# Mixers' and embedding's transposes by VectorE and DRAM into dense tiles, 64-row products in alternating halves, gate columns later

## The chip, the core and the metric

The kernel runs on one core of one Trainium2 chip. The metric is the device time of one launch in microseconds, as the median of repeated runs. PE is TensorE's matmul queue and PEld its weight loads; DVE is VectorE, ACT ScalarE, POOL GpSimd, SP the engine whose queue issues all DMA transfers here.

## The reference, cut to what matters

Two layers run over 256 tokens of width 1024. Each layer is a feed-forward half step, two token mixers side by side, a second feed-forward half step and a gated embedding:

```
x = x + 0.5 * swiglu(rmsnorm(x), ffn1)
z = rmsnorm(x) @ w_in                 # mlstm q,k,v,o,i,f ; swa q,k,v ; gates ga, gb
A = (sigmoid(o) * rmsnorm(mlstm(q,k,v,i,f))) @ w_a   # 4 heads, q and k 64 wide, v 128 wide
B = attention(rms(q), rms(k), v, window 128, sinks) @ w_b   # 8 q heads, 2 kv heads, 64 wide
x = x + (sigmoid(ga) * A + sigmoid(gb) * B) @ w_out
x = x + 0.5 * swiglu(rmsnorm(x), ffn2)
x = x + sigmoid(rmsnorm(x) @ w_ple_gate) * (p[i] @ w_ple)
```

## The kernel before, in words

The 256 tokens are two tiles (t = 0, 1) of 128 partitions. Every weight product runs in three matmuls (L230 to L232): weights and activations are split into a high and a low part (`hi`, `lo`), and high times low, low times high and high times high are summed in PSUM. Weights come as units of 1 MB. `load_next` issues a unit's DMA into one of three buffers (`raw`), ScalarE casts the high part (L202) and VectorE subtracts it for the low part (L203) into one of four buffers. `take` keeps four units ahead, so the DMA of a unit waits until VectorE is done with the unit three before, and its cast waits until PE is done with the unit four before. `stream` runs a unit for both token tiles; one tile's share is 12 matmuls of 512 columns, and behind each share `tick()` moves every waiting generator by one `yield`.

All small work of the mixers sits in such generators. A `W_` number counts the ticks that a generator waits before its next step, and so it sets how many shares of weight matmuls PE has between asking for a result and using it. PE's instructions stand in the order of the code; VectorE, ScalarE and SP run their own queues in an order that a scheduler wrote when the program was built. Each queue runs in order: a waiting instruction holds all that stand behind it.

The stages of the mixers are the projections sq, if, mqk, mv, mo, ga0, ga1, gb0, gb1 (28 ticks from mqk on), then the products with `w_a` (`ya`) and `w_b` (`yb`), then `w_out`. Beside the projections run two chains. The attention chain: normalise q and k, transpose them (`tps`, `tpk`), logits (`lg`, 64 rows of contraction, kv head 0 in partitions 0 to 63 and kv head 1 in 64 to 127), bias and softmax on DVE and ACT, transpose the probabilities (`pt`), multiply by v (`ov`), transpose the result (`tp_hb`) into `abT`. The mLSTM chain: transpose q and k (`tpq`), gates in rows, a matrix of decays `E01`, `E2` times the products of q and k (`st`, 64 rows), times v (`num`), normalise, gate, transpose (`tp_ha`) into `abT`. `drain()` runs what is left of both chains before `ya`.

Those transposes are PE instructions with the identity, followed by a copy out of PSUM. The feed-forward stages already transpose in another way (`turn`, L256): VectorE transposes 32 x 32 blocks (`inq`), SP writes them to DRAM (`scr`), SP reads them back in the wanted order (`back`), and a copy or a split moves `back` to its place.

Of the kernel before, what the change touches and what calls it, by code (L numbers as in the profile page):

```python
# [8 lines left out]
F32 = mybir.dt.float32  # L9
# [43 lines left out]
W_NORM = 5  # L53
W_CP = 6
# [6 lines left out]
W_HA = 5  # L61
# [3 lines left out]
def trunk_kernel(ctx: ExitStack, tc: tile.TileContext, a: dict, out: bass.AP):  # L65
# [99 lines left out]
    for i in range(DEPTH):  # L165
        specs.extend(ffn_specs(a["ffn1_wi"][i], a["ffn1_wo"][i], f"f1{i}"))
        for z, cols in Z.items():
            specs.extend(by_cols(a["w_in"][i], D, cols, f"z{i}_{z}"))
        for n in range(2):
            cols = [(512 * n, 512 * (n + 1))]  # L170
            specs.extend(by_cols(a["w_a"][i], 512, cols, f"wa{i}_{n}"))
            specs.extend(by_cols(a["w_b"][i], 512, cols, f"wb{i}_{n}"))
# [343 lines left out]
    def mix_in(pool, i, xn, finish):  # L516
# [21 lines left out]
        qk = pair([P, 10, HD], "qk")  # L538
# [3 lines left out]
        qT = pool.tile([P, 2, S], F32, name=f"qT{i}")  # L542
        kT = pool.tile([P, 2, S], F32, name=f"kT{i}")
# [3 lines left out]
        ha = pair([P, MLH, P], "ha")  # L547
# [20 lines left out]
        def ep_mqk(t, o, rstd):  # L568
            z = work.tile([P, 512], F32, tag="sg", name=f"mqk{i}_{t}")
            nc.scalar.activation(z, o, AF.Copy, scale=rstd)  # L570

            def turn():
                yield
                tp = bank(f"tpq{i}_{t}")
                for b in range(4):
                    nc.tensor.transpose(tp[:, b * P : (b + 1) * P], z[:, b * P : (b + 1) * P], ident)
                tv = tp.rearrange("p (b s) -> p b s", s=P)
                tok = slice(t * P, (t + 1) * P)
                nc.vector.tensor_copy(qT[:, :, tok], tv[:, 0:2, :])
                nc.vector.tensor_scalar(kT[:, :, tok], tv[:, 2:4, :], HD**-0.5, None, ALU.mult)  # L580

            spawn(turn())
# [12 lines left out]
        def swa(t):  # L595
            for _ in range(t):
                yield
            sq = pool.tile([P, 10, HD], F32, tag="s4", name=f"sqk{i}_{t}", bufs=4)
            nc.scalar.activation(sq, qk[t], AF.Square)
            s10 = small.tile([P, 10], F32, tag="s10", name=f"s10_{i}_{t}")  # L600
            nc.vector.reduce_sum(s10, sq, axis=AX.X)
            v10 = small.tile([P, 10], F32, tag="v10", name=f"v10_{i}_{t}")
            nc.vector.tensor_scalar(v10, s10, 1.0 / HD, EPS, ALU.mult, ALU.add)
            r10 = small.tile([P, 10], F32, tag="r10", name=f"r10_{i}_{t}")
            pow_neg_half(r10, v10, 10)
            z = pool.tile([P, 5 * P], F32, tag="s4", name=f"qkn{i}_{t}", bufs=4)
# [14 lines left out]
            for _ in range(W_NORM):  # L621
                yield
            tp = bank(f"tps{i}_{t}")
            for j in range(4):
                nc.tensor.transpose(tp[:, j * P : (j + 1) * P], z[:, j * P : (j + 1) * P], ident)
            nc.scalar.activation(qTs[t], heads(tp, P), AF.Copy, scale=qs)
            tk = bank(f"tpk{i}_{t}")
            nc.tensor.transpose(tk[:, 0:P], z[:, 4 * P :], ident)
            nc.scalar.activation(kTs[:, t * P : (t + 1) * P], tk[:, 0:P], AF.Copy, scale=qg[:, 1:2])
            for h0 in range(0, SWQ, 4 * (2 - t)):  # L630
                spawn(swa_part(t, h0))

        def swa_part(t, h0):
# [3 lines left out]
            nh = SWQ if t == 0 else SWQ // SWKV  # L637
            part = slice(h0, h0 + nh)
# [5 lines left out]
            yield  # L644
            L = pool.tile([P, nh, nk], F32, tag="s4", name=f"L{nmp}", bufs=4)
            mx = stat("mx")
            for j0 in range(0, nh, per):
                g = (h0 + j0) // 4
                rows = slice(HD * g, HD * (g + 1))
                o = heads(bank(f"lg{nmp}_{j0}"), nk)  # L650
                for j in range(per):
                    nc.tensor.matmul(
                        o[:, j, :], qTs[t][rows, (h0 + j0 + j) % 4, :], kTs[rows, 0:nk], start=True, stop=True
                    )
                js = slice(j0, j0 + per)
                nc.vector.tensor_tensor(L[:, js, :], o, bias[:, h0 + j0 : h0 + j0 + per, boff:], op=ALU.add)
                nc.vector.reduce_max(mx[:, js], L[:, js, :], axis=AX.X)
# [18 lines left out]
            for kt in range(t + 1):  # L676
                for j0 in range(0, nh, 4):
                    tp = bank(f"pt{nmp}_{kt}_{j0}")
                    for j in range(4):
                        nc.tensor.transpose(  # L680
                            tp[:, j * P : (j + 1) * P], L[:, j0 + j, kt * P : (kt + 1) * P], ident
                        )
                    dst = PT[:, kt, j0 : j0 + 4, :]
                    if kt + j0 == 0:
                        nc.scalar.copy(dst, heads(tp, P))
                    else:
                        nc.vector.tensor_copy(dst, heads(tp, P))
# [20 lines left out]
            hi, lo = abT[t][1]  # L708
            transpose_split(hb, nh * HD // P, hi[:, ks, :], lo[:, ks, :], f"hb{nmp}")
# [10 lines left out]
        ln, lf, F, c, M, emt = (row(n) for n in ("ln", "lf", "F", "c", "M", "emt"))  # L720

        def ml_gates():
# [19 lines left out]
            nc.vector.scalar_tensor_tensor(lf, gf, 0.0, F, ALU.min, ALU.subtract)  # L742
            nc.vector.tensor_tensor(lf, lf, c, op=ALU.add)
            nc.vector.tensor_tensor_scan(F, ones4, lf, 0.0, op0=ALU.mult, op1=ALU.add)
# [4 lines left out]
            for _ in range(W_CP):  # L749
                yield  # L750
            cp = bank(f"cp{i}")
# [5 lines left out]
            tc.keep_in_program_order(nc.sync.dma_start(scr, M))  # L757
            for _ in range(W_MB):
                yield
            spread = bass.AP(tensor=s0.tensor, offset=s0.offset, ap=[[0, P], [S, MLH], [1, S]])  # L760
            tc.keep_in_program_order(nc.sync.dma_start(Mb, spread))

        def ml_mix():
# [12 lines left out]
            for par in range(2):  # L776
                rows = slice(HD * par, HD * (par + 1))
                o = bank(f"st0{i}_{par}").rearrange("p (h t s) -> p h t s", t=2, s=P)
                for hh in range(2):
                    nc.tensor.matmul(o[:, hh], kT[rows, hh, 0:P], qT[rows, hh, :], start=True, stop=True)  # L780
                for hh in range(2):
                    ev = E01[:, 0:2, 2 * hh + par, :]
                    nc.vector.tensor_tensor(ev, ev, o[:, hh], op=ALU.mult)
                o = heads(bank(f"st1{i}_{par}")[:, 0 : 2 * P], P)
                for hh in range(2):
                    nc.tensor.matmul(o[:, hh], kT[rows, hh, P:S], qT[rows, hh, P:S], start=True, stop=True)
                for hh in range(2):
                    ev = E2[:, 2 * hh + par, :]
                    nc.vector.tensor_tensor(ev, ev, o[:, hh], op=ALU.mult)
            for t in range(NT):  # L790
                yield
                spawn(ml_out(t, E01, E2))

        def ml_out(t, E01, E2):
# [5 lines left out]
            jn = pool.tile([P, P], F32, tag="jn", name=f"jn{i}_{t}", bufs=1)  # L800
# [33 lines left out]
            hi, lo = abT[t][0]  # L834
            transpose_split(haf, 4, hi, lo, f"ha{i}_{t}")
# [81 lines left out]
    for i in range(DEPTH):  # L917
# [6 lines left out]
        with tc.tile_pool(name=f"ple{i}", bufs=1, side="right", reuse_waits="tile") as pool:  # L924
            pT = [halves(pool, 2, f"pT{i}_{t}") for t in range(NT)]

            def embed(_):
# [5 lines left out]
                for t in range(NT):  # L933
                    transpose_split(pin[t], 2, pT[t][0], pT[t][1], f"p{i}_{t}")
# [85 lines left out]
```

## Time and profile before

| | |
|---|---|
| median of three runs | 1127.14 us (1127.10 to 1127.16) |
| the profiled execution's own time | 1129.26 us |
| its span | 1127.5 us |
| PE busy in the span | 1117.9 us (99%) |
| DVE, ACT busy | 731.2 us (65%), 586.2 us (52%) |
| chain of work that ended last | PE 98%, DVE 1% |

The profiled execution took 2.1 us more than the median run, of which 1.8 us lie outside its span. A busy PE counts a matmul until its modelled end, and neighbours overlap, so the mean of one matmul is not what it costs; the distance from one start to the next is.

### The profile page before, as it was taken

Reading aid. Unit: us, or ns where it says so; the run is one execution under the profiler, and the core shown is the slowest. Engines: PE = TensorE matmul, PEld = TensorE weight load, DVE = VectorE, ACT = ScalarE, POOL = GpSimd, SP = SyncE. Lnnn points to the kernel's source line nnn. Section 1 sums busy time; section 2 is a strip of 40 time slices with the busy share of each in tenths; the row PEclk is TensorE's granted clock in tenths of the full one; section 3 lists DMA queues with packets and bytes.
Section 4 is the critical chain, followed back from the end, with each engine's and each line's share of the span. In section 5 each row is a group of like instructions: output and inputs, shape, how many; then the busy total and the mean of one; then the engine's idle time right before and its main releaser. Section 6 shows DMA issues by size and latency. Waiting matters only on the chain.

```text
span 1127.5 us, 13561 instructions
## 1 busy us (share of the span) xinstructions
PE 1117.9 (99%) x5220; PEld 929.3 (82%) x5220; DVE 731.2 (65%) x924; ACT 586.2 (52%) x848; POOL 30.5 (3%) x30
## 2 busy tenths in 40 slices
PE   8999999999999999999999999999999999999998
PEld 6788888888888888888888888888888888888887
DVE  5775755686676667656676666557846766667554
ACT  6543544667645544434664454447865364445442
POOL 1000000100000000000000000001000000000000
PEclk9999999999999999999999999999999999999999
DMA  7887766643554767756657776665544557776661
GB/s 256 277 278 248 247 214 198 224 168 113 179 191 151 261 217 246 256 190 230 208 177 246 256 238 207 224 201 188 170 148 154 193 185 226 247 238 228 218 205 38
DMA packets 147489, 235.05 MB, mean 208 GB/s; under 512 B 13288, under 2 KB 51296, under 8 KB 147424
## 3 DMA queue, kind: packets, MB, share of 16 engines
q1 hardware_dynamic: 147424, 234.19, 63.2%
q8 instruction: 41, 0.67, 0.2%
q14 instruction: 24, 0.20, 0.1%
HBM read 219.46 MB, written 14.70 MB: 208 GB/s over the span
## 4 chain that ended last, share of the span: by engine, by line
PE 98%; DVE 1%; DMA 0%; ACT 0%; issue 0%; SPq 0%
PE h_f L231 14%; PE h_f L230 14%; PE h_f L232 14%; PE acc_f_o L230 7%; PE acc_f_o L231 7%; PE acc_f_o L232 7%; PE z_mix_ga L230 1%; PE z_mix_ga L232 1%; PE z_mix_ga L231 1%; PE acc_wout L230 1%; PE z_mix_gb L230 1%; PE acc_wout L232 1%; PE z_mix_gb L232 1%; PE acc_wout L231 1%; PE z_mix_gb L231 1%; PE acc_pg L230 1%
## 5 line engine op out<-in xcount | busy, mean ns | idle before, releaser
L203 DVE TENSOR_TENSOR lo_f<-raw_f,hi_f 128x1024 fp32r<-128x1024 f32 (+1 forms) x176 | 207.6, 1216 | 97.6 <-ACT hi_f L202 97.6
L202 ACT CAST hi_f<-raw_f 128x1024 fp32r<-128x1024 f32 (+1 forms) x178 | 176.5, 1039 | 157.0 <-PE h_f L232 96.6
L203 DVE TENSOR_TENSOR lo_f_o<-raw_f_o,hi_f_o 128x1024 fp32r<-128x1024 f32 x88 | 104.2, 1219 | 73.6 <-ACT hi_f_o L202 73.6
L231 PE MATMUL h_f<-hi_f,xT_f_0l 128*128 128x512 f32 x352 | 137.8, 392 | 2.3 <-DVE xT_f_0l L247 2.3
L230 PE MATMUL h_f<-lo_f,xT_f_0h 128*128 128x512 f32 x352 | 138.6, 394 | 0.1
L230 PE MATMUL h_f<-lo_f,xT_f_1h 128*128 128x512 f32 x352 | 137.2, 390 | 0.6 <-DVE lo_f L203 0.5
L232 PE MATMUL h_f<-hi_f,xT_f_0h 128*128 128x512 f32 x352 | 137.5, 391 | 0.0
L232 PE MATMUL h_f<-hi_f,xT_f_1h 128*128 128x512 f32 x352 | 137.0, 389 | 0.0
L231 PE MATMUL h_f<-hi_f,xT_f_1l 128*128 128x512 f32 x352 | 137.0, 389 | 0.0
L202 ACT CAST hi_f_o<-raw_f_o 128x1024 fp32r<-128x1024 f32 x88 | 88.0, 1048 | 91.5 <-PE acc_f_o L232 55.0
L231 PEld LDWEIGHTS h_f<-hi_f,xT_f_0l 128*128 128x128 f32 x352 | 66.5, 189 | 16.0 <-DVE xT_f_0l L247 2.6
L230 PEld LDWEIGHTS h_f<-lo_f,xT_f_1h 128*128 128x128 f32 x352 | 66.1, 188 | 15.1 <-DVE lo_f L203 1.4
L230 PEld LDWEIGHTS h_f<-lo_f,xT_f_0h 128*128 128x128 f32 x352 | 66.4, 189 | 14.5 <-issue 0.6
L232 PEld LDWEIGHTS h_f<-hi_f,xT_f_0h 128*128 128x128 f32 x352 | 66.6, 189 | 14.0
L232 PEld LDWEIGHTS h_f<-hi_f,xT_f_1h 128*128 128x128 f32 x352 | 66.0, 188 | 13.7
L231 PEld LDWEIGHTS h_f<-hi_f,xT_f_1l 128*128 128x128 f32 x352 | 66.1, 188 | 13.5
L232 PE MATMUL acc_f_o<-hi_f_o,hT_f_1h 128*128 128x512 f32 x176 | 68.5, 389 | 0.0
L230 PE MATMUL acc_f_o<-lo_f_o,hT_f_0h 128*128 128x512 f32 x176 | 68.5, 389 | 0.0
L231 PE MATMUL acc_f_o<-hi_f_o,hT_f_0l 128*128 128x512 f32 x176 | 68.5, 389 | 0.0
L232 PE MATMUL acc_f_o<-hi_f_o,hT_f_0h 128*128 128x512 f32 x176 | 68.5, 389 | 0.0
L230 PE MATMUL acc_f_o<-lo_f_o,hT_f_1h 128*128 128x512 f32 x176 | 68.5, 389 | 0.0
L231 PE MATMUL acc_f_o<-hi_f_o,hT_f_1l 128*128 128x512 f32 x176 | 68.5, 389 | 0.0
(363 smaller groups left out, 2042.3 us busy)
## 6 DMA issues: line engine op xcount, KB each, us to landing
raw_f<-in_ffn_wi_dram SPq DMA_DIRECT2D x79, 1024.0 KB, 5.3
raw_f_o<-in_ffn_wo_dram SPq DMA_DIRECT2D x40, 1024.0 KB, 5.2
scr_h_f<-inq_h_f SPq DMA_DIRECT2D x40, 256.0 KB, 3.5
back_h_f<-scr_h_f SPq DMA_DIRECT2D x40, 256.0 KB, 4.4
raw_f<-in_ffn_wi_dram SPq DMA_DIRECT2D x18, 512.0 KB, 4.5
raw_z_ga<-in_w_in_dram SPq DMA_DIRECT2D x8, 1024.0 KB, 5.4
raw_z_gb<-in_w_in_dram SPq DMA_DIRECT2D x8, 1024.0 KB, 5.2
raw_wout<-in_w_out_dram SPq DMA_DIRECT2D x8, 1024.0 KB, 5.0
```

What stands on the lines that cost most here:

```text
L202: nc.scalar.copy(hi[:, o:e], raw[:, o:e])
L203: (nc.gpsimd if between and o // step % 2 == 0 else nc.vector).tensor_tensor(lo[:, o:e], raw[:, o:e], hi[:, o:e].bitcast(F32), op=ALU.subtract
L230: nc.tensor.matmul(o, xh, wl[:, k, sl], start=start, stop=False)
L231: nc.tensor.matmul(o, xl, wh[:, k, sl], start=False, stop=False)
L232: nc.tensor.matmul(o, xh, wh[:, k, sl], start=False, stop=stop)
```

## The change

`back_from` runs `turn` for the mixers' blocks, and what was a PE transpose and a copy out of PSUM becomes a VectorE transpose, two DMAs and a copy (or split) out of SBUF into the same dense tiles. Per layer this holds for `tps` and `tpk` (2 turns of 640 columns), `tpq` (2 of 512), `pt` (6 of 512), `tp_hb` (one of 512, two of 256), `tp_ha` (2 of 512) and the embedding's `tp_p` (2 of 256). The transposes of `x` (`tp_f`, `tp_mix`, `tp_ple`), of the merged mixers (`tp_mx`) and of the gates (`gp`, `cp`) stay with PE. The logits of both kv heads and the `st` products of both partition halves alternate, each half in its own PSUM bank. `scr0<-M` and its spread are issued before the gate columns (`cp`), `yb` comes before `ya`, and the waits in ticks are set anew. Some tiles share buffers (`qk` with `ha`, `lf` with `ln`).

```diff
-W_NORM = 5
-W_CP = 6
+W_NORM = 2
+W_MQ = 2
+W_ROW = 7
-W_HA = 5
+W_HA = 3
...
+        def back_from(src, name):
+            k = src.shape[1]
+            inq = work.tile([P, 5 * P], F32, tag="xg", name=f"inq_{name}")
+            back = pool.tile([P, 5 * P], F32, tag="back", name=f"back_{name}", bufs=2)
+            b = back[:, 0 : k * P].rearrange("p (a e) -> p a e", a=4)
+            yield from turn(inq, src, b, name)
+            return b.rearrange("p a (k s) -> p k a s", s=32)
...
-                        nc.tensor.transpose(
-                            tp[:, j * P : (j + 1) * P], L[:, j0 + j, kt * P : (kt + 1) * P], ident
-                        )
+                b = yield from back_from(src, f"PT{nmp}_{kt}_{j0}")
...
+            for k0 in range(0, 4, per):
+                os = [heads(bank(f"lg{i}_{t}_{k0}_{g}"), nk) for g in range(SWKV)]
+                for j in range(per):
+                    for g in range(SWKV):
+                        rows = slice(HD * g, HD * (g + 1))
+                        nc.tensor.matmul(
+                            os[g][:, j, :], qTs[t][rows, k0 + j, :], kTs[rows, 0:nk], start=True, stop=True
+                        )
...
-            transpose_split(hb, nh * HD // P, hi[:, ks, :], lo[:, ks, :], f"hb{nmp}")
+            yield from back_split(blocks(hb), hi, lo, f"hb{nmp}")
...
-            transpose_split(haf, 4, hi, lo, f"ha{i}_{t}")
+            yield from back_split(blocks(haf), *abT[t][0], f"ha{i}_{t}")
...
         for n in range(2):
+            ob = [bank(f"yb{i}_{t}_{n}") for t in range(NT)]
+            stream(ob, abTs, [f"wb{i}_{n}_0"], 4, kbase=4)
             oa = [bank(f"ya{i}_{t}_{n}") for t in range(NT)]
             stream(oa, abTs, [f"wa{i}_{n}_0"], 4)
-            ob = [bank(f"yb{i}_{t}_{n}") for t in range(NT)]
-            stream(ob, abTs, [f"wb{i}_{n}_0"], 4, kbase=4)
```

On PE, the products of mLSTM's q and k in layer 0 stood behind a transpose of attention's result and in one half after the other (`st00_0` and `st10_0` read partitions 0 to 63, `st00_1` and `st10_1` 64 to 127):

```order
L253 MATMUL tp_hb0_1_0_2267<-ident_85,hb0_1_0_2234 128x128 x2
L253 MATMUL tp_hb0_1_4_2272<-ident_85,hb0_1_4_2245 128x128 x2
L780 MATMUL st00_0_2277<-qT0_1561,kT0_1562 128x256 x2
L786 MATMUL st10_0_2282<-qT0_1561,kT0_1562 128x128 x2
L780 MATMUL st00_1_2287<-qT0_1561,kT0_1562 128x256 x2
L786 MATMUL st10_1_2292<-qT0_1561,kT0_1562 128x128 x2
```

These are the same products in the change:

```order
L807 MATMUL st00_0_2217<-qkT0_1561 128x256
L807 MATMUL st00_1_2218<-qkT0_1561 128x256
L807 MATMUL st00_0_2217<-qkT0_1561 128x256
L807 MATMUL st00_1_2218<-qkT0_1561 128x256
L815 MATMUL st10_0_2227<-qkT0_1561 128x128
L815 MATMUL st10_1_2228<-qkT0_1561 128x128
L815 MATMUL st10_0_2227<-qkT0_1561 128x128
L815 MATMUL st10_1_2228<-qkT0_1561 128x128
```

The transposes are gone from here, and the halves alternate product by product.

On DVE, in the stretch of gb0 in layer 0, this stood between attention's last product with v and the split of its transposed result (`hb0_1_0` and `hb0_1_4` are the two kv heads of token tile 1, `abT0_1_1l` is what `yb` of tile 1 reads):

```order
L702 TENSOR_TENSOR hb0_1_0_2234<-ov0_1_0_2225,rinv0_1_0_2042 128x256
L702 TENSOR_TENSOR hb0_1_4_2245<-ov0_1_4_2236,rinv0_1_4_2069 128x256
L247 TENSOR_TENSOR abT0_0_1l_1534<-tp_hb0_0_0_2218,abT0_0_1h_1533 128x512
L203 TENSOR_TENSOR lo_z0_gb0_0_2249<-raw_z0_gb0_0_2247,hi_z0_gb0_0_2248 128x1024 x2
L783 TENSOR_TENSOR E01_0_2190<-E01_0_2190,st00_0_2277 128x2x128 x2
L247 TENSOR_TENSOR abT0_1_1l_1538<-tp_hb0_1_0_2267,abT0_1_1h_1537 128x256
```

Now the same two ends stand farther apart, with both round trips of token tile 0 between them:

```order
L729 TENSOR_TENSOR hb0_1_4_2457<-ov0_1_4_2448,rinv0_1_4_2094 128x256
L264 STREAM_TRANSPOSE inq_ha0_0_2459<-ha0_0_2237 128x512
L264 STREAM_TRANSPOSE inq_hb0_1_0_2476<-hb0_1_0_2446 128x256
L248 TENSOR_TENSOR abT0_0_1l_1534<-back_hb0_0_0_2435,abT0_0_1h_1533 128x512
L204 TENSOR_TENSOR lo_wb0_0_0_2489<-raw_wb0_0_0_2487,hi_wb0_0_0_2488 128x1024 x2
L264 STREAM_TRANSPOSE inq_hb0_1_4_2479<-hb0_1_4_2457 128x256
L264 STREAM_TRANSPOSE inq_ha0_1_2484<-ha0_1_2238 128x512
L204 TENSOR_TENSOR lo_wa0_0_0_2535<-raw_wa0_0_0_2533,hi_wa0_0_0_2534 128x1024 x2
L248 TENSOR_TENSOR abT0_0_0l_1532<-back_ha0_0_2460,abT0_0_0h_1531 128x512
L204 TENSOR_TENSOR lo_wb0_1_0_2574<-raw_wb0_1_0_2572,hi_wb0_1_0_2573 128x1024 x2
L248 TENSOR_TENSOR abT0_1_1l_1538<-back_hb0_1_0_2477,abT0_1_1h_1537 128x256
L248 TENSOR_TENSOR abT0_1_1l_1538<-back_hb0_1_4_2480,abT0_1_1h_1537 128x256
```

What moved: the split for tile 1 of `yb` now stands behind two splits that wait for transfers from DRAM and behind six weight splits.

On SP, the queue held in this place only weights (`raw_`), one after another; now, in the same place of layer 0, it reads:

```order
L270 DMA scr_hb0_1_0_2507<-inq_hb0_1_0_2476 128x256
L199 DMA raw_wa0_1_0_2614<-in_w_a_dram 128x4x512
L270 DMA scr_hb0_1_4_2509<-inq_hb0_1_4_2479 128x256
L270 DMA scr_ha0_1_2511<-inq_ha0_1_2484 128x512
L274 DMA back_ha0_0_2460<-scr_ha0_0_2482 128x4x128
L274 DMA back_hb0_1_0_2477<-scr_hb0_1_0_2507 128x4x64
L199 DMA raw_wout0_0_2648<-in_w_out_dram 128x2x1024
L274 DMA back_hb0_1_4_2480<-scr_hb0_1_4_2509 128x4x64
```

Writes to and reads from DRAM stand between the weights, and a weight that waits for its buffer holds them.

## Rows read from the trace of the kernel before

**Rows 1.** The page: the chain that ended last, share of the span by engine.
```profile
PE 98%; DVE 1%; DMA 0%; ACT 0%; issue 0%; SPq 0%
```
**Rows 2.** The chain in order of time: start us, length us, what.
```profile
218.96 0.44 PE gp L727 x4
...
238.15 1.64 PE lg L652 x16
...
242.73 2.90 PE lg L652 x16
...
254.97 1.75 PE pt L680 x16
...
264.46 3.52 PE ov L694 x32
```
**Rows 3.** PE's transposes by form: count, then busy us and mean ns.
```profile
L680 PE MATMUL pt<-ident,L 128*128 128x128 f32 x48 | 5.9, 272 | 0.0
...
L625 PE MATMUL tps<-ident,qkn 128*128 128x128 f32 x16 | 2.4, 272 | 0.0
...
L253 PE MATMUL tp_p<-ident,pin 128*128 128x128 f32 x8 | 1.2, 271 | 0.0
L628 PE MATMUL tpk<-ident,qkn 128*128 128x128 f32 x4 | 1.1, 272 | 0.0
```
**Rows 4.** Timeline of PE, 271 to 282: start us, length us, line, what.
```profile
271.17 1.13 PE L780 MATMUL st<-qT,kT 64*128 64x256 f32 x4
272.14 0.27 PE L786 MATMUL st<-qT,kT 64*128 64x128 f32 x1
272.15 0.48 PE L780 MATMUL st<-qT,kT 64*128 64x256 f32 x1
...
273.11 0.60 PE L786 MATMUL st<-qT,kT 64*128 64x128 f32 x4
...
276.50 0.39 PE L230 MATMUL z_mix_ga<-lo_z_ga,xT_mix_0h 128*128 128x512 f32 x1
...
281.26 0.39 PE L230 MATMUL z_mix_ga<-lo_z_ga,xT_mix_0h 128*128 128x512 f32 x1
```
**Rows 5.** DVE's groups by form: count, then busy us and mean ns.
```profile
L203 DVE TENSOR_TENSOR lo_z_gb<-raw_z_gb,hi_z_gb 128x1024 fp32r<-128x1024 f32 x16 | 19.2, 1220 | 11.3 <-ACT hi_z_gb L202 11.3
...
L263 DVE STREAM_TRANSPOSE inq_h_f<-hh_f 128x256 f32<-128x256 f32 x8 | 5.0, 631 | 0.1
...
L825 DVE SCALAR_TENSOR_TENSOR ha<-ha,rn,mlg 128x128 f32<-128x128 f32 x16 | 4.6, 347 | 4.0 <-POOL rn L301 4.0
L263 DVE STREAM_TRANSPOSE inq_mix<-x 128x512 f32<-128x512 f32 x4 | 4.4, 1106 | 0.1
...
L831 DVE TENSOR_TENSOR ha<-ha,gates 128x512 f32<-128x512 f32 x4 | 2.8, 688 | 0.0
...
L702 DVE TENSOR_TENSOR hb<-ov,rinv 128x256 f32<-128x256 f32 x4 | 1.7, 425 | 10.0 <-PE ov L694 10.0
```
**Rows 6.** Window; busy us of PE, PEld, DVE, ACT, POOL; clock; DMA.
```profile
224.00:252.00 28.00, 28.00 (x151) 23.00 (x149) 24.02 (x50) 17.84 (x46) 2.76 (x1) 1.00 0.50 169
```
**Rows 7.** Timeline of DVE: the first sum of tile 1's logits and bias.
```profile
244.70 0.68 DVE L656 TENSOR_TENSOR L<-lg,bias 128x512 f32<-128x512 f32 x1
```
**Rows 8.** Line L269, the DRAM writes of turns: all 56, issue to landing.
```profile
DMA to landing us min/median/max: 2.2/3.5/6.0
```
**Rows 9.** Line L273, the DRAM reads of turns: all 56, issue to landing.
```profile
DMA to landing us min/median/max: 2.2/3.1/7.4
```
**Rows 10.** DMA issues: count, KB each, median us to landing.
```profile
back_h_f<-scr_h_f SPq DMA_DIRECT2D x40, 256.0 KB, 4.4
```
**Rows 11.** POOL's group of the power that normalises mLSTM's result.
```profile
L301 POOL TENSOR_TENSOR rn<-vn,half_neg 128x4 f32<-128x4 f32 x4 | 4.9, 1220 | 128.1 <-DVE vn L821 128.1
```
**Rows 12.** PE's longest wait: us in total, times, longest.
```profile
PE h_f L231 <- DVE xT_f_0l L247: 2.3, 1, 2.3
```
**Rows 13.** Window behind that wait, columns as in rows 6.
```profile
12.00:14.00 2.00, 2.00 (x6) 1.60 (x5) 1.01 (x5) 0.30 (x2) 1.08 (x2) 0.50 1.05 387
```

More of the change, by code (lines that the diff above doesn't have):

```diff
@@ L536, in pair, with over_qk @@
             return [pool.tile(shape, F32, name=f"{name}{i}_{t}") for t in range(NT)]
-        qk = pair([P, 10, HD], "qk")
+        def over_qk(shape, name):
+            return [pool.tile(shape, F32, tag=f"qk{t}", name=f"{name}{i}_{t}") for t in range(NT)]
+        qk = over_qk([P, 10, HD], "qk")
         vsw = pair([P, P], "vsw")
@@ L546, in mix_in, with quarters, back_split @@
         kTs = pool.tile([P, S], F32, name=f"kTs{i}")
-        ha = pair([P, MLH, P], "ha")
+        def back_from(src, name):
[5 more added lines that the diff above has]
+            return b.rearrange("p a (k s) -> p k a s", s=32)
+        def quarters(ap):
+            return ap.rearrange("p k (a s) -> p k a s", s=32)
+        def back_split(src, hi, lo, name):
+            b = yield from back_from(src, name)
+            split_evac(quarters(hi), quarters(lo), b)
         def project(z, epilogue):
@@ L570, in ep_mqk, with turned @@
             nc.scalar.activation(z, o, AF.Copy, scale=rstd)
[L572 to L582, printed above, removed]
+            def turned():
+                for _ in range(W_MQ):
+                    yield
+                b = yield from back_from(blocks(z), f"mqk{i}_{t}")
+                d = quarters(qkT[:, :, t * P : (t + 1) * P])
+                nc.vector.tensor_copy(d[:, 0:2], b[:, 0:2])
+                nc.vector.tensor_scalar(d[:, 2:4], b[:, 2:4], HD**-0.5, None, ALU.mult)
+            spawn(turned())
         def ep_mv(t, o, rstd):
@@ L622, in swa, with swa_logits @@
                 yield
[L623 to L633, printed above, removed]
+            b = yield from back_from(blocks(z), f"qk{i}_{t}")
+            nc.scalar.activation(quarters(qTs[t]), b[:, 0:4], AF.Copy, scale=qs)
+            kt = kTs[:, t * P : (t + 1) * P].rearrange("p (a s) -> p a s", s=32)
+            nc.scalar.activation(kt, b[:, 4], AF.Copy, scale=qg[:, 1:2])
+            spawn(swa_logits(t))
+        def swa_logits(t):
+            yield
             nk = P * (t + 1)
@@ L637, in swa_part @@
             nh = SWQ if t == 0 else SWQ // SWKV
+            parts = []
+            for h0 in range(0, SWQ, nh):
+                nmp = f"{i}_{t}_{h0}"
+                L = pool.tile([P, nh, nk], F32, tag="s4", name=f"L{nmp}", bufs=4)
+                mx = small.tile([P, nh], F32, tag=f"mx{t}{h0}", name=f"mx{nmp}", bufs=1)
+                parts.append((h0, L, mx))
+            for k0 in range(0, 4, per):
[6 more added lines that the diff above has]
+                        )
+                for g in range(SWKV):
+                    head = 4 * g + k0
+                    h0, L, mx = parts[head // nh]
+                    js = slice(head - h0, head - h0 + per)
+                    nc.vector.tensor_tensor(L[:, js, :], os[g], bias[:, head : head + per, boff:], op=ALU.add)
+                    nc.vector.reduce_max(mx[:, js], L[:, js, :], axis=AX.X)
+            for h0, L, mx in parts:
+                gen = swa_part(t, h0, nh, L, mx)
+                spawn(gen)
+                advance(gen)
+        def swa_part(t, h0, nh, L, mx):
             part = slice(h0, h0 + nh)
@@ L707, in swa_part @@
             ks = slice(h0 * HD // P, (h0 + nh) * HD // P)
-            hi, lo = abT[t][1]
-            transpose_split(hb, nh * HD // P, hi[:, ks, :], lo[:, ks, :], f"hb{nmp}")
+            hi, lo = (part[:, ks, :] for part in abT[t][1])
+            yield from back_split(blocks(hb), hi, lo, f"hb{nmp}")
         cem = small.tile([P, 16], F32, tag="cem", name=f"cem{i}")
@@ L748, in ml_gates @@
             nc.scalar.activation(emt, emt, AF.Exp, scale=-1.0)
-            for _ in range(W_CP):
+            for _ in range(W_ROW):
                 yield
+            tc.keep_in_program_order(nc.sync.dma_start(scr, M))
+            for _ in range(W_MB):
+                yield
+            spread = bass.AP(tensor=s0.tensor, offset=s0.offset, ap=[[0, P], [S, MLH], [1, S]])
+            tc.keep_in_program_order(nc.sync.dma_start(Mb, spread))
             cp = bank(f"cp{i}")
@@ L775, in ml_mix, with ml_out @@
                 yield
[L776 to L781, printed above, removed]
+            half = [slice(HD * par, HD * (par + 1)) for par in range(2)]
+            os = [bank(f"st0{i}_{par}").rearrange("p (h t s) -> p h t s", t=2, s=P) for par in range(2)]
+            for hh in range(2):
+                for o, rows in zip(os, half):
+                    nc.tensor.matmul(o[:, hh], qkT[rows, 2 + hh, 0:P], qkT[rows, hh, :], start=True, stop=True)
+            for hh in range(2):
+                for par, o in enumerate(os):
                     ev = E01[:, 0:2, 2 * hh + par, :]
                     nc.vector.tensor_tensor(ev, ev, o[:, hh], op=ALU.mult)
[L784 to L787, printed above, removed]
+            os = [heads(bank(f"st1{i}_{par}")[:, 0 : 2 * P], P) for par in range(2)]
+            for hh in range(2):
+                for o, rows in zip(os, half):
+                    nc.tensor.matmul(o[:, hh], qkT[rows, 2 + hh, P:S], qkT[rows, hh, P:S], start=True, stop=True)
+            for hh in range(2):
+                for par, o in enumerate(os):
                     ev = E2[:, 2 * hh + par, :]
                     nc.vector.tensor_tensor(ev, ev, o[:, hh], op=ALU.mult)
+            ha = over_qk([P, MLH, P], "ha")
             for t in range(NT):
                 yield
-                spawn(ml_out(t, E01, E2))
-        def ml_out(t, E01, E2):
+                spawn(ml_out(t, ha, E01, E2))
+        def ml_out(t, ha, E01, E2):
             for _ in range(W_NUM):
@@ L799, in ml_out @@
             ssn = small.tile([P, MLH], F32, tag="ssn", name=f"ssn{i}_{t}")
-            jn = pool.tile([P, P], F32, tag="jn", name=f"jn{i}_{t}", bufs=1)
+            jn = work.tile([P, 512], F32, tag="junk", name=f"jn{i}_{t}", bufs=1)[:, 0:P]
             for hp in range(2):
@@ L933, in embed @@
                 for t in range(NT):
-                    transpose_split(pin[t], 2, pT[t][0], pT[t][1], f"p{i}_{t}")
+                    inq = work.tile([P, 5 * P], F32, tag="xg", name=f"inq_p{i}_{t}")
+                    yield from turn_split(pool, inq, blocks(pin[t]), *pT[t], f"p{i}_{t}")
             ffn(xn, f"f2{i}", behind(nxt, 0.5, W_F2), embed)
```

51 lines of the change are left out of this document (15 added, 36 removed).

## The prediction

> **What bounds the kernel now.** I read the chain of waits first. It shows PE on 98% of the span [rows 1], so whatever PE issues is paid one for one, and other engines cost only what they make PE wait. Then the same chain in order of time, for what one PE instruction takes of the path: sixteen transposes take 1.75 us [rows 2], 109 ns each. The groups by form then tell how many there are [rows 3], the timeline how PE works on half arrays [rows 4], and VectorE's groups and a window what the new work meets [rows 5, 6]. The profiled execution took 1129.26 us, 2.1 us above the median of the runs; the sum below is a difference worked out in that execution and taken off the median, 1127.1.
>
> **What PE loses.** Over both layers 48 transposes of probabilities, four groups of 16 (`tps`, `tpq`, `tp_ha`, `tp_hb`), 8 of the embedding and 4 of `tpk` go: 124 [rows 3]. At 109 ns [rows 2] that is **13.5 us**. The mean in the groups is 272 ns [rows 3], but neighbours overlap, and the chain counts 109.
>
> The Trainium skill, "TensorE: Matmul & The Clock Gate", Part 4: PE-mode transpose, puts a transpose in a kernel at about 275 ns. Rows 3 agree with it as a duration, rows 2 do not as a price; by the page the term would be 34.1 us, by the rows it is 13.5.
>
> **What PE gains on half arrays.** The `st` products of the lower and the upper half already meet once: a 128-column pass of the one starts at 272.14, a 256-column pass of the other at 272.15 [rows 4], so the two halves do run at the same time. Where no switch is near, the pairs run alone. With halves alternating, each pair should take the time of one. Logits: 1.64 us to about 0.85, and 2.90 to 1.75 [rows 2] (eight 256-column passes at 0.215, the pitch that 1.13 us for four with a first start and a tail gives). `st`: from 271.17 to 273.71 is 2.5 us [rows 4], to about 1.5. Together 2.95 per layer, **5.9 us** in two. Bounds: nothing, if pairs of this shape do not overlap, and 7.0, half of what both layers spend there (7.04 each). I take 5.9, since the overlap is in the rows.
>
> So PE's own work shrinks by 19.4 us. Order of `yb` and `ya`, shared buffers and the later gate columns add no PE work; they matter only through waits.
>
> **What is added.** Per layer 14 round trips besides the embedding's two: 2 of 640 columns, 10 of 512, 2 of 256. VectorE pays 1.11 us for 512 and 0.63 for 256 [rows 5], so an estimated 1.34 for 640: 15.0 us per layer. It is rid of reads out of PSUM but does the same copies and splits out of SBUF, priced the same (0.69 and 0.42 [rows 5]). SP gets 28 more issues per layer in its queue. A landing takes 2.2 to 6.0 us for the write, median 3.5 [rows 8], and 2.2 to 7.4 for the read, median 3.1 [rows 9] (4.4 for the 256 KB reads of the feed-forward stage alone [rows 10]). This is free where PE asks late enough. One share of weight matmuls, 12 of them, is 2.72 us (21 starts lie 4.76 us apart [rows 4]). Two places look short; in the others, the first logits, the `ov` products and the weight units, I find slack of 2 us or more or a wait under half a microsecond, and count nothing.
>
> *The decays, before `num`.* From 224 to 252 VectorE is busy 24.0 of 28 us [rows 6]. Four transposes now fall there (2 x 1.34 + 2 x 1.11 = 4.9 us): it is full. The first sum of tile 1's logits stood at 244.70 [rows 7] and comes at about 249.6. PE, from the gates' end at 219.4 [rows 2], has eight shares (21.8), the first logits (1.0), a share and the gate columns with the second logits (2.2): it ends these at 247.1, so VectorE is 2.5 us behind. From there to the first two products with `E01` VectorE has four sums and four maxima, two preparations of `E01` and `E2` (ten of 0.69), six transposes (6.6), four copies and two products (six of 0.42), two weight splits (2.4) and a dozen tiny ones (about 1.2): 19.6 us [rows 5]. PE has seven shares and `st`: 19.0 + 1.5 = 20.5. Late by 2.5 + 19.6 - 20.5 = 1.6; I take **1.5 us** a layer. Bounds: nothing, if the 4.0 idle us of the window take the transposes in; 4, if another 2.5 us of waits for ScalarE fall in. Queued behind VectorE here are the weight splits of gb0, which PE wants only 8 us later.
>
> *Attention's last result, before `yb` of tile 1.* From the last `ov` product to `yb` of tile 1 PE has eight shares, 21.8 us. VectorE reaches `hb0_0_0` only after the last copy of probabilities, the statistics, POOL's power (1.2 [rows 11]), four products of 0.35 and one of 0.69 [rows 5], 3.2 us, while PE is still half of 3.5 us [rows 2] in `ov`: it starts 1.4 us after `ov` ends. Then up to the two `abT0_1_1l` it does eight weight splits (9.8), three transposes of 512 and two of 256 (4.6), and small ones: four of 0.69, four of 0.42, four of 0.35 (5.8) [rows 5], less 0.4 for neighbours that overlap: 19.8. Between stand two waits for DRAM. After the first transpose a round trip of 3.5 + 3.1 and 1.0 for issue and cast is covered by 6.8 of work: 0.8 open. After the last transpose, three issues, a read of 3.1 and the cast (4.5) meet two weight splits (2.4): 2.1 open. Sum 1.4 + 19.8 + 0.8 + 2.1 = 24.1, late by **2.3 us** a layer. Bounds: 0.6 with the shortest landings, 4.9 with reads of 4.4, 13.4 with the longest of both. I stay with the medians, since the feed-forward's 4.4 is read where weights flow without a pause, and here the DMA share is 0.50 [rows 6].
>
> The embedding's two turns have the whole second feed-forward to land. The sum: 19.4 - 2 x (1.5 + 2.3) = 11.8 us off 1127.1, **1115.3 us**.
>
> **The rivals.** *All of it hidden.* If VectorE absorbs its transposes in its idle time and the landings are short, PE never waits and the time is 1127.1 - 19.4 = 1107.7. For it speaks that the feed-forward stages hide the same round trips: PE's longest wait in the whole trace is 2.3 us, near the start [rows 12]. Against it, the full window [rows 6]. Chance 0.22.
>
> *Half arrays do not pair.* The passes of one pair write two banks and load two sets of weights each time; the rows show overlap only at one switch. Then the sum is 1121.2. Chance 0.08.
>
> *The reads wait behind weights.* On SP the read for tile 1 stands behind a weight that waits for its buffer, and that buffer is freed by a VectorE split which itself stands behind a read. If landings are near the longest, 6.0 and 7.4 [rows 8, 9], `yb` is 13.4 us late a layer and the time 1127.1 - 19.4 + 2 x (1.5 + 13.4) = 1137.5. It decides, that is, the kernel becomes slower, from 9.7 us of waits a layer on, with `num` at 1.5 from 8.2 at `yb`. A long wait also costs clock: after PE's 2.3 us wait [rows 12] the granted clock was 0.50, the 1.2 GHz level, for the window shown [rows 13], whose 2 us hold six matmul starts, where at the pitch of rows 4 they would hold nine; so about a microsecond more per wait. Chance of slower 0.11, and of eating the gain up to no change 0.10.
>
> *A transpose costs its duration.* 124 x 272 ns is 33.7 us; then 1127.1 - 33.7 - 5.9 + 7.6 = 1095.1. It would need PE to stand still in each, and the chain shows eight and sixteen running into the next product. Chance 0.03.
>
> **How the numbers follow.** My case, 1110.5 to 1122, has 0.46: both waits at the low bounds (1.2 us in two layers) give about 1109, with 4 and 4.9 us 1125.5, and I cut the outer ends. A measurement here tells 0.2%, 2.3 us. Faster by more: 0.46 + 0.22 + 0.08 + 0.03 = 0.79; within: 0.10; slower: 0.11. The range that leaves out two in ten goes from 1107, with the hidden case, to 1126, which takes in the unpaired one and part of the waits.
>
> **What would show it.** PE's groups: 124 transposes fewer, `lg` and `st` starting in pairs a few ns apart. PE's waits: `num` on DVE `E01` for about 1.5 us and `yb` on DVE `abT` for about 2.3 us, twice each, and none of such size elsewhere. VectorE up by about 32 us busy in the span, DMA by 15 MB. Wrong would be: no PE waits (hidden), `lg` at its old length (unpaired), or waits on weight splits `lo_`, which would mean that SP's or VectorE's queue delays weights, which I count as covered.

## The result, and the profile after

The changed kernel takes 1118.84 us (median; runs 1118.42 to 1120.08) against 1127.15 beside it: 0.9926 of the time, 95% interval 0.9913 to 0.9938. That is 8.3 us faster, where 11.8 were forecast. A later set of runs of the same kernel gave 1115.72 (1114.91 to 1117.33), 0.990 (0.9887 to 0.9913): most runs of the kernel before lie within a microsecond of each other, those of the changed one do not.

The profiled executions show where most of the 3 us between the two sets lies. It is at the start of the kernel, which the change leaves alone. The first matmul on `xT_f_0l` and the first products of the gates (`gp`), in the first profiled execution, then in that of the later set:

```profile
11.45 0.50 PE L232 MATMUL h_f<-hi_f,xT_f_0l 128*128 128x512 f32 x1 [2.21 <-DVE xT_f_0l L248]
...
218.97 0.60 PE L754 MATMUL gp<-ident,gz 128*4 128x128 f32 x4
```

```profile
10.07 0.50 PE L232 MATMUL h_f<-hi_f,xT_f_0l 128*128 128x512 f32 x1 [1.25 <-DVE xT_f_0l L248]
...
216.48 0.60 PE L754 MATMUL gp<-ident,gz 128*4 128x128 f32 x4
```

PE waits a microsecond longer in the first, and from 11 to 16 us its granted clock is 0.66 in the mean, against 1.00 in the second. Each trace has 968 PE instructions ahead of `gp`, and so has the kernel before, whose `gp` starts at 218.80 behind a wait of 2.27 us, a late start too. From the start of `gp` to the end of the span, the three take 908.7 (before), 897.6 and 896.6 us. So like for like the change is worth 11.1 to 12.1 us. The 8.3 of the first medians is too low if the other runs of the changed kernel in that set began late as well, for which there is no trace. Below, "from the gates on" means this stretch of the profiled execution.

The first profiled execution took 1118.42 us, 10.8 less than that of before. Its page, first the span, then busy time by engine, then the chain's shares by engine (it answers to [rows 1]):

```profile
span 1116.6 us, 13467 instructions
...
PE 1104.3 (99%) x5096; PEld 913.7 (82%) x5096; DVE 756.7 (68%) x958; ACT 585.7 (52%) x848; POOL 29.6 (3%) x30
...
PE 80%; DVE 11%; DMA 4%; issue 2%; ACT 2%; POOL 1%; SPq 0%; DVEq 0%
```

PE lost 124 instructions (5220 before), the number of transposes removed. The chain, 98% PE before, now leaves PE for VectorE and DMA. PE's waits (us in total, times, longest) show where:

```profile
PE yb L232 <- DVE abT_1l L248: 1.2, 2, 1.0
PE yb L231 <- ACT abT_1h L247: 1.1, 1, 1.1
...
PE lg L664 <- DVE L L671: 0.5, 2, 0.2
...
PE ya L232 <- DVE abT_0l L248: 0.2, 1, 0.2
```

None of these is in the list of before. The wait for `abT` was forecast, that of `num` for `E01` is absent, and one at the second logits is new. PE's timeline of the logits of the first layer in the kernel before (start, length; the chain of [rows 2] has each 0.06 or 0.07 shorter, since it counts from the end of the work ahead):

```profile
238.08 1.71 PE L652 MATMUL lg<-kTs,qTs 64*128 64x128 f32 x16
...
242.66 2.96 PE L652 MATMUL lg<-kTs,qTs 64*128 64x256 f32 x16
```

and of the 64-row products after the change (answers to [rows 2, 4]):

```profile
241.29 1.16 PE L664 MATMUL lg<-kTs,qTs 64*128 64x128 f32 x16
...
245.67 1.56 PE L664 MATMUL lg<-kTs,qTs 64*128 64x256 f32 x10
247.47 1.13 PE L664 MATMUL lg<-kTs,qTs 64*128 64x256 f32 x6 [0.24 <-DVE L L671]
...
259.63 1.14 PE L807 MATMUL st<-qkT 64*128 64x256 f32 x8
260.60 0.61 PE L815 MATMUL st<-qkT 64*128 64x128 f32 x8
```

The first logits fell from 1.71 to 1.16 us and `st` from 2.54 to 1.58, but the second logits, from 245.67 to 248.60, still take 2.93, as before. After ten of the sixteen PE stands still until VectorE has summed. VectorE's timeline says why the sum is late:

```profile
242.79 2.36 DVE L204 TENSOR_TENSOR lo_z_ga<-raw_z_ga,hi_z_ga 128x1024 fp32r<-128x1024 f32 x2 [0.98 <-ACT hi_z_ga L203]
245.59 1.23 DVE L204 TENSOR_TENSOR lo_z_ga<-raw_z_ga,hi_z_ga 128x1024 fp32r<-128x1024 f32 x1 [0.44 <-ACT hi_z_ga L203]
246.73 1.28 DVE L671 TENSOR_TENSOR L<-lg,bias 128x512 f32<-128x512 f32 x2
```

The first logits ended at 242.45, and their sums come at 246.73, behind three weight splits that wait for ScalarE's casts.

For `num` the rows that matter are the first sum of tile 1's logits and the products with `E01` on VectorE, and PE's `num`:

```profile
250.60 1.28 DVE L671 TENSOR_TENSOR L<-lg,bias 128x512 f32<-128x512 f32 x2
...
266.63 1.39 DVE L811 TENSOR_TENSOR E<-E,st 128x256 f32<-128x256 f32 x4
```

```profile
269.44 1.05 PE L838 MATMUL num<-vaug,E 128*128 128x129 f32 x8
```

VectorE is 2.0 us behind PE's second logits, as forecast within half a microsecond, but is done with the four products at 268.02, 1.4 us before PE asks.

The end of the mixer in the second layer, PE's timeline:

```profile
855.17 0.39 PE L233 MATMUL yb<-hi_wb,abT_1h 128*128 128x512 f32 x1
856.65 0.50 PE L231 MATMUL yb<-lo_wb,abT_1h 128*128 128x512 f32 x1 [1.09 <-ACT abT_1h L247]
858.14 0.50 PE L232 MATMUL yb<-hi_wb,abT_1l 128*128 128x512 f32 x1 [0.98 <-DVE abT_1l L248]
...
859.11 0.63 PE L232 MATMUL yb<-hi_wb,abT_1l 128*128 128x512 f32 x1
859.54 0.63 PE L233 MATMUL yb<-hi_wb,abT_1h 128*128 128x512 f32 x1
...
862.10 0.41 PE L233 MATMUL yb<-hi_wb,abT_1h 128*128 128x512 f32 x1
862.35 0.39 PE L231 MATMUL ya<-lo_wa,abT_0h 128*128 128x512 f32 x1
```

Two gaps, and then starts 0.43 us apart instead of 0.227. The window behind them (busy us of PE, PEld, DVE, ACT, POOL, then the granted clock and DMA) shows a granted clock of 0.50, the lower level of 1.2 GHz, after two waits of about a microsecond:

```profile
858.70:862.00 3.30, 3.30 (x9) 2.61 (x8) 2.63 (x3) 1.58 (x2) 0.00 (x0) 0.50 0.91 315
```

From 855.17 to 862.35 there are 13 starts; at 0.227 they take 2.95 us, so this place costs 4.2. In the first layer, from 307.53 to 315.48 with 27 starts, `yb` and `ya` together cost 1.8.

What is `abT` late for? SP's queue in the first layer (start, length of issue):

```profile
293.14 0.56 SPq L270 DMA_DIRECT2D scr_ha<-inq_ha  x1
293.81 0.37 SPq L270 DMA_DIRECT2D scr_hb<-inq_hb  x1
...
298.34 0.32 SPq L270 DMA_DIRECT2D scr_hb<-inq_hb  x1
299.30 0.32 SPq L270 DMA_DIRECT2D scr_ha<-inq_ha  x1
299.67 0.45 SPq L274 DMA_DIRECT2D back_ha<-scr_ha  x1
300.21 0.55 SPq L274 DMA_DIRECT2D back_hb<-scr_hb  x1
...
305.14 0.36 SPq L274 DMA_DIRECT2D back_hb<-scr_hb  x1
...
308.30 0.36 SPq L274 DMA_DIRECT2D back_ha<-scr_ha  x1
```

and VectorE's timeline beside it:

```profile
297.68 0.63 DVE L264 STREAM_TRANSPOSE inq_hb<-hb 128x256 f32<-128x256 f32 x1 [1.20 <-DMA scr_ha<-inq_ha]
...
304.42 0.69 DVE L248 TENSOR_TENSOR abT_0l<-back_ha,abT_0h 128x512 fp32r<-128x512 f32 x1 [2.91 <-ACT abT_0h L247]
```

The third transpose waits 1.2 us, not for its data but for a slot of `xg` that the write of `ha` still holds. The first read of `ha`, whose write went out at 293.14, goes out at 299.67, behind the two writes that this wait made late. The third read goes at 305.14, when `abT_0l` has emptied one of the two slots of `back`, and the fourth at 308.30. So the last reads go out late for want of slots, on top of what DRAM takes; the experiments put that to the test.

### The profile page after: what moved, and what is told of

Read it like the earlier page. It is cut to its first block, busy times and chain, and to the rows that moved or that the text cites. A ratio compares the mean times of both kernels' runs of the same rounds, so it can differ in the third digit from the quotient of the medians.

```text
span 1116.6 us, 13467 instructions
## 1 busy us (share of the span) xinstructions
PE 1104.3 (99%) x5096; PEld 913.7 (82%) x5096; DVE 756.7 (68%) x958; ACT 585.7 (52%) x848; POOL 29.6 (3%) x30
## 4 chain that ended last, share of the span: by engine, by line
PE 80%; DVE 11%; DMA 4%; issue 2%; ACT 2%; POOL 1%; SPq 0%; DVEq 0%
PE h_f L232 14%; PE h_f L231 14%; PE h_f L233 14%; PE acc_f_o L232 7%; PE acc_f_o L233 7%; PE acc_f_o L231 7%; DMA back_PT<-scr_PT 2%; PE acc_wout L233 1%; PE acc_wout L231 1%; PE acc_wout L232 1%; PE acc_pg L233 1%; PE acc_pg L231 1%; PE acc_pg L232 1%; DVE lo_z_ga L204 1%; DVE inq_PT L264 1%
```

## The experiments

Each ran beside the kernel before, whose median was 1127.12 to 1127.62 in the four sets. Times are medians, with their runs in brackets, then the ratio to the kernel before and its 95% interval. No run of the changed kernel stands beside the first four, and executions can differ by the 2.5 us of the start, so the figure from the gates on is given too: 897.6 and 896.6 us for the changed kernel.

### The halves one after the other

```diff
-                for j in range(per):
-                    for g in range(SWKV):
+                for g in range(SWKV):
+                    for j in range(per):
```

and the same exchange of loops in both groups of `st`.

> The changed kernel, but the 64-row products of the logits and of mLSTM's scores go one half after the other again; everything else stays. The prediction put the alternation at 5.9 us, so the time should rise from 1118.8 to about 1124.7. The trace after shows first logits 1.16 us long, the second 2.93 with a wait in the midst and scores 1.58, against 1.64, 2.90 and 2.5 before, so 1.4 us a layer: by that the time rises only to about 1121.7. If the halves do not run side by side at all it stays at 1118.8.

Measured 1117.03 (1116.26 to 1119.27), 0.991 (0.9897 to 0.9922), 898.0 from the gates on: between the two sets of the changed kernel, and 0.4 to 1.4 us slower from the gates on. Both numbers were wrong, and the time alone would speak for no pairs. Its timeline of PE:

```profile
243.76 2.10 PE L664 MATMUL lg<-kTs,qTs 64*128 64x256 f32 x16
```

The second logits take 2.10 without alternation. The edit had left the new grouping, two banks at a time, and with it three switches between halves in the second logits, and PE's list of waits has none there. `st` kept three switches too. What it undid was not the change's part; the run `own_old_order` below does that.

### Only the alternation, in the kernel before

The new `swa_logits` and the new loops of `st` are put into the kernel before; PE's transposes stay.

> The kernel before, with PE's transposes kept, and only the order of the 64-row products changed to alternate halves. Prediction's term: 5.9 us less, 1121.2. If the second logits lose their pairing after the change only because VectorE's sums come late there, they pair here, where VectorE is ahead, and 5.9 is seen in full. If the pairing is broken by the banks of PSUM whatever VectorE does, the second logits keep about 2.9 us and the gain is about 2.9: 1124.2.

Measured 1124.22 (1124.17 to 1125.14), 0.9971 (0.996 to 0.9982), 905.8 from the gates on, 2.9 less than before. By the time alone that is the theory of the banks. The trace says otherwise:

```profile
236.75 1.16 PE L651 MATMUL lg<-kTs,qTs 64*128 64x128 f32 x16
...
240.79 2.00 PE L651 MATMUL lg<-kTs,qTs 64*128 64x256 f32 x16
```

The pairs hold throughout, 2.00 for 2.96, and with 1.16 for 1.71 and 1.58 for 2.54 in `st` that is 4.9 us of work in two layers. About 2 were given back: PE now waits for ScalarE's exponentials amid the transposes of probabilities (`pt`, four times, 0.7 us in all), and in the first layer, the waits included, 5.57 us pass from the second `pt` to `ov` where 4.51 did before.

### Own slots for mLSTM's turns

```diff
+            if own:
+                inq, back = own(name)
...
+                both.append(pool.tile([P, MLH, S], F32, tag="Mb", name=f"inqs{i}"))
+            back = pool.tile([P, 4, P], F32, tag=f"qTs{t}", name=f"back_{name}")
```

> The changed kernel, but the two round trips of mLSTM's result get slots of their own in tiles that are dead by then (inq in that of the spread rows, back in that of the turned queries), so they no longer share xg and back with hb. Theory: VectorE's late transposes wait 1.2 us for a slot that a DRAM write holds, and SP issues the reads behind them, so yb and ya wait; with own slots the reads go 2 us or more earlier and most of the waits at yb and ya (about 2 us in the first layer, 4 in the second with the lowered clock) go: 1113 to 1115. Rival: the reads are late because of landing times and of weights ahead of them on SP; then 1118 to 1119.5.

Measured 1114.49 (1113.35 to 1118.39), 0.9895 (0.9879 to 0.9912), 895.0 from the gates on, 1.6 to 2.6 less. The median is where the slots' theory has it, but it was reckoned from 1118.8; from the later set's 1115.72 the gain is 1.2, and two runs stay at 1118.4. So this run alone speaks for the slots without showing them. PE still waits at `yb`, 1.3 and 0.4 us, for reads of `hb`.

### `hb` and `ha` by PE again

```diff
-            yield from back_split(blocks(hb), hi, lo, f"hb{nmp}")
+            transpose_split(hb, nh * HD // P, hi, lo, f"hb{nmp}")
-            yield from back_split(blocks(haf), *abT[t][0], f"ha{i}_{t}")
+            transpose_split(haf, 4, *abT[t][0], f"ha{i}_{t}")
```

> The changed kernel, but hb and ha are turned by PE as before, one share later (W_HB 2, W_HA 4): 16 transposes a layer come back, at 109 ns 3.5 us in all, and the waits at yb and ya go with the round trips. If these waits cost what the trace shows, about 6 us with the clock, the time falls to about 1116. If they would be lost elsewhere anyway, it rises by the 3.5 to about 1122.

Measured 1115.99 (1114.62 to 1118.11), 0.9899 (0.9886 to 0.9911), 897.3 from the gates on. The number came as expected, but like for like nothing was gained (897.6 and 896.6 for the changed kernel). The waits at `yb` and `ya` are gone from its list; the transposes (3.5 us at 109 ns) and 1.6 us of a new wait at `tp_hb`, for VectorE's `hb`, took their place.

### The changed kernel again

> The changed kernel, unaltered, as the measure for the runs beside it: 1118.4 to 1120.1. If its waits at yb and ya depend on how long DRAM takes to land in an execution, its second trace shows them at other lengths than the first (about 2 us in the first layer, 4 in the second) and its runs scatter by 1 to 2 us.

Measured 1115.72 (1114.91 to 1117.33). The trace has waits at the same places (`yb` 1.2 and 0.4, `ya` 1.0 and 0.5), and the scatter of 2.4 us is a little over what was expected; its level, 3 us below the first set, was not expected. Between the two profiled executions, 3.5 us apart, 2.5 are the start and 1.0 the second layer's waits.

### Own slots for all late turns

`hb`'s `inq` goes into the tile of the turned queries and keys (`qkT`), and the two reads of tile 1 share one slot of `back`.

> As the kernel with mLSTM's turns in slots of their own, and hb's turns too: their inq in the tile of the turned mLSTM queries and keys, the two reads of tile 1 in one slot. With mLSTM's turns alone in own slots the trace still shows a read of hb behind a slot and yb waiting 1.3 and 0.4 us in the two layers together, with the clock about 3.3 us. If slots are the cause, the rest goes too: about 1110 to 1112, with little scatter. If what is left is the landing of the last DRAM write and read, it stays at 1113 to 1115.

Measured 1110.20 (1110.03 to 1112.68), 0.9856 (0.9842 to 0.987), 891.9 from the gates on. PE's waits in the mixers, whole:

```profile
PE lg L677 <- DVE L L684: 0.5, 2, 0.3
```

SP's queue: the three reads of `hb` and the last of `ha` go out together at last.

```profile
298.83 1.47 SPq L274 DMA_DIRECT2D back_hb<-scr_hb  x3
300.41 0.45 SPq L274 DMA_DIRECT2D back_ha<-scr_ha  x1
```

That the want of slots made `yb` and `ya` late is thereby shown: same transposes, same bytes, same queue, and 4.7 to 5.7 us less from the gates on (5.5 to 8.6 in the medians). Two things moved with the slots. The scheduler, free of them, set the first transpose of `ha` 4.7 us earlier, counted from the gates. And `ha`'s landings were shorter, 2.9 us for the write and 3.4 for the read against 4.5 and 5.1 in the changed kernel; but the last kernel below has 4.5 and 6.0 with own slots and PE waits nowhere in its mixers.

### `cp` later, alone and with own slots

```diff
-W_ROW = 7
+W_ROW = 8
```

> The changed kernel with one number changed: W_ROW 8 for 7, which sets the four small transposes cp (and the issues of the row ahead of them) one share later, behind the second logits. Theory: cp takes a bank of PSUM, so that the fourth bank of the second logits is one that VectorE has yet to read out, and its late sum breaks the alternation; without cp ahead the 2.93 us of the second logits fall to about 1.75, and the time by 2 us, to about 1117. Rival: VectorE's lateness alone sets the end of these products; then they keep 2.9 us and the time stays within half a microsecond of the unaltered kernel.

> Both of these edits together, own slots for ha and hb and cp later. They act at different places, so the gains should add: about 1108 to 1110, near the 1107.7 at which nothing waits. If a faster PE only runs into the same landing of the last reads, the cp edit adds nothing and the time is that of the kernel with own slots.

Alone 1118.30 (1115.55 to 1120.62), 0.9921 (0.9909 to 0.9934); with own slots 1111.21 (1108.81 to 1113.67), 0.9858 (0.9842 to 0.9874). The place did what was said; alone, PE's timeline:

```profile
242.86 2.00 PE L664 MATMUL lg<-kTs,qTs 64*128 64x256 f32 x16
```

0.9 us less, with VectorE as late as ever (its first sum comes 4.3 us after the first logits end, in the changed kernel too): it was the bank, not the lateness alone. But the time did not follow: alone it was 2.6 us above the changed kernel beside it. PE reached `ov` earlier and waited there, 2.5 us in the two layers, for the last copies of probabilities, and 3.6 at `yb`. With own slots too (PE's timeline, first layer, of a run that took 1113.67):

```profile
279.23 2.12 PE L734 MATMUL ov<-vsw,PT 128*128 128x64 f32 x18
283.01 3.25 PE L734 MATMUL ov<-vsw,PT 128*128 128x64 f32 x14 [1.67 <-DVE PT L724]
```

and from 282 to 290 the granted clock was 0.57 in the mean. Two of its four runs took 1108.8 and 1108.9. My sum of gains overlooked `ov` as next in line.

### Slots for the last reads of probabilities too

```diff
+            back = pool.tile([P, 4, P], F32, tag=f"qTs{kt}", name=f"back_{name}")
```

> Own slots for ha and hb and cp later, as in the run that gave 1108.8 twice and 1113.5 twice, and slots of their own for the last two reads of probabilities (the tiles of the turned queries, dead by then). There PE waited 1.7 us or more at ov for the last copy of probabilities, and the second pair of these reads stood behind the two slots of back. If the slots cause it, the wait goes and all runs come to 1108.3 to 1109. If the DRAM landing itself is late, the runs still scatter between 1108.8 and 1113.5.

Measured 1108.72 (1108.63 to 1108.83), 0.9833 (0.982 to 0.9847): the best version, 890.2 from the gates on, 6.4 to 7.4 below the changed kernel. The runs lie within 0.2 us. Chain by engine:

```profile
PE 97%; DVE 1%; DMA 1%; issue 0%; ACT 0%; SPq 0%
```

### The old order of the products

In the kernel with own slots for `ha` and `hb`, the loops stand as in the kernel before: all of one half, then all of the other.

> The kernel with own slots for ha and hb (1110.2, no wait of PE in the mixers but at the second logits), with the loops over the 64-row products exactly as in the kernel before: all of one half, then all of the other, so one switch in each group instead of one at each product. The earlier run with the halves in turn kept the new grouping by banks and so still switched three times in the second logits and in the scores. Prediction's term: 5.9 us more, 1116.1. From the traces: first logits 1.64 for 1.16, second 2.90 for about as much (the wait for a bank spoils the pairs now), scores 2.5 for 1.58, so about 1.5 us a layer: 1113.2. If pairs are worth nothing: 1110.2.

Measured 1114.29 (1113.09 to 1115.59), 0.9879 (0.9864 to 0.9894): 2.9 us more in the lower two runs, 4.1 in the median. The profiled execution is one of the upper two and began late (`gp` at 219.07); from the gates on it takes 894.7, 2.8 more than the kernel with own slots. The logits have 1.71 and 2.96 us again:

```profile
241.39 1.71 PE L677 MATMUL lg<-kTs,qTs 64*128 64x128 f32 x16
...
246.33 2.96 PE L677 MATMUL lg<-kTs,qTs 64*128 64x256 f32 x16
```

### What a transpose costs

> The same kernel with own slots, and the probabilities turned by PE again: 48 transposes in both layers come back (W_PT 4 for 3, the ov products stay where they are), and 12 round trips with their 12 VectorE transposes of 1.1 us go. Where nothing waits for VectorE, a transpose's price is all that counts: at 109 ns 5.2 us more, 1115.4; at the 272 ns of its duration 13.1 more, 1123.3. If VectorE's 13 us were still on the path, the time would rise by less than 3 or fall.

Measured 1132.41 (1131.22 to 1132.89), 1.0042 (1.003 to 1.0055): none of the three. It was put badly: the transposes stand straight ahead of `st`, which then waits for banks that their copies hold, and those stand behind exponentials on ScalarE. PE's waits:

```profile
PE st L821 <- DVE PT L726: 4.5, 2, 2.3
PE st L821 <- ACT PT L724: 2.0, 2, 1.2
PE st L829 <- ACT PT L724: 1.2, 2, 0.9
```

Of 22.2 us more, 5.2 of transposes (at 109 ns) and 7.7 of waits leave 9 open; a granted clock of 0.66 from 260 to 270 and 0.83 from 270 to 280 goes with part of it. So the price was measured by itself, in the best version:

```diff
-W_HB = 1
+W_HB = 4
...
-            yield from back_split(blocks(hb), hi, lo, f"hb{nmp}", lambda name: hb_slots(t, h0, name))
+            transpose_split(hb, nh * HD // P, hi, lo, f"hb{nmp}")
```

> The price of a transpose, where nothing else waits: the kernel of 1108.7, whose four runs lie within 0.2 us, with hb alone turned by PE again, late enough that neither PE nor yb waits for it (W_HB 4). 16 transposes in both layers come back in four groups. At 109 ns each the time rises by 1.7 us to 1110.5; at the 272 ns of a transpose's duration by 4.4 to 1113.1; if PE's transposes ran wholly beside other work, it stays at 1108.7. The earlier try with the probabilities cost 22 us, because the scores then waited for banks of PSUM that the copies of probabilities had not yet given back, so it said nothing on this price.

Measured 1110.39 (1109.94 to 1110.65), 0.9843 (0.9829 to 0.9857): 1.67 us for 16 transposes, 104 ns each, and 1.8 from the gates on (892.0 for 890.2). By the extremes of both kernels' runs the price lies between 69 and 126 ns, far from 272.

## Why the prediction was right, and where its sizes were off

**The sum came out, in part by luck.** 11.8 us were forecast; like for like the traces have 11.1 and 12.1. But the half arrays gave 2.8 us less than forecast, and the wait at `num`, 3.0 us in two layers, did not come: two errors that cancel. The terms follow.

**The transposes: right.** 13.5 us stood in the sum; at the measured 104 ns they are 12.9. The Trainium skill, "TensorE: Matmul & The Clock Gate", Part 4: PE-mode transpose, gives about 275 ns for one; the traces agree with it as a duration (272, [rows 3]), but as a price it would have put the last run at 1113.1, and it came at 1110.4.

**The half arrays: mechanism right, the term mis-sized.** 5.9 us stood in the sum; the lines of the changed kernel give 0.55 + 0.03 + 0.96 a layer, 3.1 in all, and putting the old order back cost 2.8 to 2.9. Two causes: a group of pairs takes longer than I took it (1.16 us for 0.85, 2.00 for 1.75), which leaves 4.9 where nothing interferes, as in the kernel before; and the second logits lost their gain to a bank that VectorE had not read out. I had VectorE 2.5 us behind at just this place and looked for the loss only at `num`.

**`num` on `E01`: wrong.** 1.5 us a layer were forecast, none came. VectorE was behind as forecast (2.0 us for 2.5) and PE took 20.8 us from there to `num` (20.5 forecast); the step that failed is VectorE's list in between, 19.6 us, which took 17.4 with all four products. The lateness cost PE only at the second logits, with 0.24 us of standing still and pairs that fall apart.

**`yb` on `abT`: right in place and nearly in size.** 2.3 us a layer, 4.6 in all, were forecast; the first trace has 1.8 and 4.2, also at `ya`. The step that failed is what I put them down to: the sum added DRAM landings to VectorE's work, one transfer after the other, and left out that the late turns share two slots of `xg` and two of `back`. With own slots landings as long were hidden. In the first layer the wait is under, in the second over the 2.3, part of it the lowered clock.

**Costs of the added work.** The prediction counted 14 round trips a layer, ten of 512 columns; there are 15, eleven of 512. VectorE was busy 25.5 us more, not 32, though its new transposes take 33.6 in DVE's groups by form: the copies out of SBUF are cheaper than those out of PSUM, which the prediction priced the same (a copy of probabilities took 0.69 us before and takes 0.43 now), and neighbours overlap. DMA moved 16.2 MB more (15 forecast).

The sum by the lines: 13.5 + 3.1 - 6.0 = 10.6, against 11.1 from the gates on. The medians differ by 8.3, since before's profiled execution was 2.1 above its median and that of the change 0.4 below. The 2.1 lie within the span, about as much as a late start costs, and not mostly outside it as the section on the time before has it: in every run the time is about 1.8 us longer than the span.

**The rivals.** All of it hidden, 1107.7, is nearly what the best version reaches: 1108.72 with no wait left in the mixers, 18.4 us below before, the 13.5 of the transposes and the 4.9 of pairs that nothing disturbs. Reads that wait behind others on SP do exist, but behind slots and for 6 us in both layers, far from the 9.7 a layer that would have made it slower. Pairs do form, and a transpose does not cost its duration.

Not tried by themselves: the exchanged order of `yb` and `ya`, the shared buffers and the new waits in ticks. Why an execution begins late stays open. Kernels without a wait of PE in the mixers scatter too, that with the old order of products from 1113.1 to 1115.6.

## What to carry to other kernels

When transposes leave a saturated engine for a round trip, count the slots that the trips share as well as their landings: here a source slot was held until the write had landed, and a read waited for a slot that a copy had yet to empty. Tiles that are dead by then served as slots without a cost in the runs. After each wait removed, ask which place is next: here the gain at the logits came back as a wait at `ov` until that had its slots too. And before two executions a few microseconds apart are compared, look where in the trace they part: here most of it was at the start, far from the change.

## What was not expected of the hardware

Products on the two halves of the array overlapped at each switch, even without strict alternation: the second logits took 2.96 us with one switch, 2.10 with three, 2.00 alternating.

What a wait costs in clock differed from one execution to the next. Behind the waits of 1.09 and 0.98 us at `yb` the granted clock was 0.50 for 3.3 us; in the second trace of the same kernel, waits of 0.38 and 0.98 at that place were followed by 1.00 (from 855 to 857). At the start PE waited 2.21 us in the first trace of the changed kernel and 2.24 in that of the alternation alone; from 11 to 16 the granted clock was 0.66 in the one and 1.00 in the other.
